# Half of a first weight group moved from ScalarE's DMA queue to the head of GpSimd's

## The chip, the cores and the metric

The kernel runs on one core of a Trainium2 chip. A core has five engines that run side by side: TensorE (matrix products), VectorE, ScalarE, GpSimd and SyncE (SP), and 16 DMA engines that move data between the device memory (HBM) and the on-chip memory (SBUF). Transfers are issued by SP, ScalarE (ACT) and GpSimd (POOL), each through a queue of its own. The metric is the device time of one execution in microseconds; before the change it is 84.93 us, the median of 7 runs (84.66 to 85.0).

## The reference

```python
batch, dim_i, dim_j, dim_k = 32, 256, 256, 128     # all float32
np.einsum('bi,bj,kij->bk', x, y, weight)
```

For every batch row b and every k the result is the bilinear form x[b] · weight[k] · y[b]. The weight is 128 x 256 x 256 float32, 33.6 MB, and is used once; x, y and the output are small.

## The kernel before

The weight is cut into G = 32 groups g. A group holds the four k with k = kk * 32 + g, kk = 0 to 3, laid out over the 128 partitions so that a partition holds eight (IC = 8) neighbouring rows i of one k, each of 256 elements j. In float32 that is 8 KB per partition and 1 MB per group. TensorE forms, for each group, the sum over i of x[b,i] * weight[k,i,j]: eight matmul steps, one per row ic, with a block matrix `xblk[:, ic]` (x spread so that the 32 batch rows meet the four k separately) as the stationary operand and the group's row ic, 256 columns, as the moving one. The result for a group is 128 x 256 float32 in PSUM, half a bank. VectorE multiplies it by y and sums over j, which gives one column of the output buffer `acc`.

Groups are worked in six units (`UNITS`) of 16, 8, 4, 2, 1 and 1 groups. Unit 0 takes the even groups and fills all eight PSUM banks; it runs its rows from ic = 7 down to 0, the next unit up, and so on. Unit 1 may start when VectorE has read unit 0's banks; units 2, 3 and 4 take banks that unit 1 does not use, and unit 5 (group 31) takes unit 1's first bank again.

The matmuls read bfloat16 from `w_sb`. Two ways lead there. Groups 0 and 16 (`FIRST`) come as plain float32 into `w_f`, group 0 through SP's queue and group 16 through ScalarE's (L134), and ScalarE casts each in two halves (L178). All the other groups come through GpSimd's queue with the cast done by the DMA itself (L120), in the order of `LOADS`: (8, 24), then (4, 12, 20, 28), then all of 2, 6, 10, ..., then unit 1's eight groups, unit 2's four, unit 3's two, group 15, and group 31 in four pieces of 4, 2, 1 and 1 rows. One transfer, y, is put between the second and third (`sw.insert(2, ...)`, L127). x goes through ScalarE's queue ahead of group 16 (L130). Every transfer has a semaphore of its own (`s_w`, `s_f`, `s_x`, `s_y`); a matmul waits for the semaphore of the load that holds its row (`sem_of`), the first time it is needed.

The order is written out by hand: the issues of all these transfers are moved to the very beginning of the program, ahead of the barrier that starts the engines (SP's and ScalarE's before anything else, GpSimd's after its start-up constants). After that GpSimd makes an identity matrix (L168, L169); VectorE repeats and transposes x (L192, L198), makes a mask from the identity (L205) and from both the block matrix (L210), then repeats and transposes y into `y4` (L219 to L227). TensorE waits for all four casts and the block matrix before its first matmul, then follows the units. At the end SP writes `acc` out, and GpSimd and SP clear the semaphores.

Of the kernel before, what the change touches and what calls it, by code (L numbers as in the profile page):

```python
# [15 lines left out]
)  # L16

LOADS = (
    ((8, 24), 0, 8),
    ((4, 12, 20, 28), 0, 8),  # L20
    (tuple(range(2, 32, 4)), 0, 8),
# [8 lines left out]
)  # L30

FIRST = (0, 16)
BANKS = 8


@with_exitstack
def kernel(
# [7 lines left out]
    nc = tc.nc  # L45
# [8 lines left out]
    _, J = y.shape  # L54
# [3 lines left out]
    IC = I // IP  # L58
# [7 lines left out]
    def sbuf(name, shape, dtype):  # L66
        return nc.alloc_sbuf_tensor(name, shape, dtype).ap()

    def rows_of(groups):


        step = G // len(groups)
        assert all(g == groups[0] + n * step for n, g in enumerate(groups))
        v = weight.rearrange("(u s) (ip ic) j -> s ip u (ic j)", s=step, ic=IC)
        return v[groups[0]]

    def w_of(groups):
        at = [place_of[g] for g in groups]
        step = at[1] - at[0] if len(at) > 1 else 1
        assert all(a == at[0] + n * step for n, a in enumerate(at))  # L80
        return w_sb[:, at[0]:at[-1] + 1:step, :]

    w_sb = sbuf("w_sb", [P, G, IC * J], bf16)
    w_f = sbuf("w_f", [P, len(FIRST), IC * J], f32)
    x_sb = sbuf("x_sb", [B, I], f32)
    y_sb = sbuf("y_sb", [B, J], f32)
# [9 lines left out]
    acc = sbuf("acc", [P, G], f32)  # L96
    ps = nc.alloc_psum_tensor("ps", [P, BANKS, 2, J], f32).ap()


    s_w = [nc.alloc_semaphore(f"w{n}") for n in range(len(LOADS))]  # L100
    sem_of = {
        (g, ic): s
        for s, (groups, lo, hi) in zip(s_w, LOADS) for g in groups for ic in range(lo, hi)
    }
    s_f = [nc.alloc_semaphore(f"f{g}") for g in FIRST]
    s_x = nc.alloc_semaphore("x")
    s_y = nc.alloc_semaphore("y")
# [11 lines left out]
    sw = [  # L119
        nc.gpsimd.dma_start(  # L120
            out=w_of(groups)[:, :, lo * J:hi * J],
            in_=rows_of(groups)[:, :, lo * J:hi * J],
        ).then_inc(s, 16).ins
        for (groups, lo, hi), s in zip(LOADS, s_w)
    ]

    sw.insert(2, nc.gpsimd.dma_start(out=y_sb, in_=y).then_inc(s_y, 16).ins)  # L127

    hw = [
        nc.scalar.dma_start(out=x_sb, in_=x).then_inc(s_x, 16).ins,  # L130
    ]
    for n, (g, queue) in enumerate(zip(FIRST, (nc.sync, nc.scalar))):
        hw.append(
            queue.dma_start(  # L134
                out=w_f[:, n:n + 1, :], in_=rows_of((g,)),
            ).then_inc(s_f[n], 16).ins
        )
    for ins in [*hw, *sw]:
# [10 lines left out]
    for blk in blocks:  # L149
# [20 lines left out]
        out=ident, in_=ident, compare_op=mybir.AluOpType.not_equal, fill=1.0,  # L170
# [3 lines left out]

    for n, g in enumerate(FIRST):
        for h in range(2):
            lo, hi = h * IC * J // 2, (h + 1) * IC * J // 2
            c = act.copy(out=w_sb[:, place_of[g], lo:hi], in_=w_f[:, n, lo:hi])  # L178
            if h == 0:
                c._wait_ge(s_f[n], 16)  # L180
            c.then_inc(s_act, 1)
# [4 lines left out]
    def done(ins):  # L186
# [6 lines left out]
        out=x_rep,  # L193
        in_=x_sb.rearrange("b (ip ic) -> b ic ip", ic=IC).unsqueeze(3)
        .to_broadcast([B, IC, IP, KK]),
    )._wait_ge(s_x, 16))
    for q in range(Q):
        c = v.transpose(  # L198
            out=xt[q * 32:(q + 1) * 32, :, :],
            in_=x_rep[:, :, q * IP // Q:(q + 1) * IP // Q, :],  # L200
# [5 lines left out]
        out=mask, in_=ident.rearrange("p (ip kk) -> p kk ip", kk=KK), axis=AX, op=add,  # L206
    )._wait_ge(s_pool, 2))

    for kk in range(KK):
        c = v.tensor_scalar(  # L210
            out=xblk[:, :, :, kk], in0=xt, scalar1=mask[:, kk:kk + 1],
# [8 lines left out]
        out=yt, in_=y_sb.rearrange("b (jb j) -> b jb j", j=32),  # L220
    )._wait_ge(s_y, 16))
    t = done(v.tensor_copy(  # L222
        out=y_rep, in_=yt.unsqueeze(3).to_broadcast([B, J // 32, B, KK]),
    )._wait_ge(s_dve, t))
    BQ = B // Q
    for q in range(Q):
        c = v.transpose(  # L227
            out=y4[q * 32:(q + 1) * 32, :].rearrange("p (jb j) -> p jb j", j=32),
            in_=y_rep[:, :, q * BQ:(q + 1) * BQ, :],
# [13 lines left out]

    pe.wait_ge(s_act, 2 * len(FIRST))
    pe.wait_ge(s_dve, t_x)
    at_dve = t_x
    n_pe = 0
    freed = [0] * BANKS
    landed = set()
    p0 = bank = 0  # L250
    held = None
    for u, unit in enumerate(UNITS):

        n_g = len(unit)
        n_b = (n_g + 1) // 2
        if bank + n_b > BANKS:
            bank = 0
# [8 lines left out]
        for n_step, (ic, h) in enumerate(steps):  # L266
            n = n_g // n_b
# [25 lines left out]
        if n_g > 1:  # L293
            t = done(v.tensor_tensor(  # L294
                out=prod, in0=sums, in1=y4.unsqueeze(1).to_broadcast([P, n_g, J]), op=mult,
# [3 lines left out]
                out=acc[:, unit[0]:unit[-1] + 1:unit[1] - unit[0]], in_=prod, axis=AX, op=add,  # L299
            )._wait_ge(s_dve, t))  # L300
        else:
            done(v.tensor_tensor_reduce(  # L302
                out=prod[:, 0, :], in0=sums[:, 0, :], in1=y4, scale=1.0, scalar=0.0,
# [44 lines left out]
```

## Time and profile before

| | |
|---|---|
| median of 7 runs | 84.93 us (84.66 to 85.0) |
| the profiled execution, and its span | 84.57 us, 83.3 us |
| TensorE busy / VectorE / ScalarE / GpSimd | 32.0 / 25.1 / 5.2 / 8.8 us |
| GpSimd's DMA queue (q0) | 4432 packets, 15.76 MB written |
| ScalarE's queue and SP's (q10, q1) | 192 and 288 packets, 1.08 and 1.07 MB written |
| read from HBM | 33.62 MB |
| issue to landing: group 0 by SP / group 16 by ScalarE / y by GpSimd | 4.8 / 8.1 / 19.6 us |
| GpSimd's issues of weight transfers | 11, at 1.06 to 9.15 us, 702 ns each in the mean |
| ScalarE's casts | 4, 1040 ns each, 7.34 to 11.22 us |
| first matmul | 41.77 us |

Times are counted from the first instruction of the span. Busy time of the engines is their compute instructions; on GpSimd the page counts the issuing of its DMAs too. GB/s and MB of a queue are bytes written, so for a casting transfer they are half of what is read. PE stands for TensorE, DVE for VectorE, ACT for ScalarE, POOL for GpSimd. L numbers are lines of the kernel before.

### The profile page before, as it was taken

Reading aid. Unit: us, or ns where it says so; the run is one execution under the profiler, and the core shown is the slowest. Engines: PE = TensorE matmul, PEld = TensorE weight load, DVE = VectorE, ACT = ScalarE, POOL = GpSimd, SP = SyncE. Lnnn points to the kernel's source line nnn. Section 1 sums busy time; section 2 is a strip of 40 time slices with the busy share of each in tenths; the row PEclk is TensorE's granted clock in tenths of the full one; section 3 lists DMA queues with packets and bytes.
Section 4 is the critical chain, followed back from the end, with each engine's and each line's share of the span. In section 5 each row is a group of like instructions: output and inputs, shape, how many; then the busy total and the mean of one; then the engine's idle time right before and its main releaser. Section 6 shows DMA issues by size and latency. Waiting matters only on the chain.

```text
span 83.3 us, 257 instructions
## 1 busy us (share of the span) xinstructions
PE 32.0 (38%) x136; PEld 4.2 (5%) x43; DVE 25.1 (30%) x28; ACT 5.2 (6%) x5; POOL 8.8 (11%) x18
## 2 busy tenths in 40 slices
PE   0000000000000000000099999994039997884780
PEld 0000000000000000000000000000000100112330
DVE  0009450000291000000000000005999602999732
ACT  0009930000000000000000000000000000000000
POOL 5999600000000000000000000000000000000000
PEclk9999999999999999999999999999975999999999
DMA  3999999999999999999999999999999999999980
GB/s 122 417 362 285 214 211 220 216 213 209 228 214 214 209 216 216 220 214 213 211 213 220 218 211 213 216 213 220 216 213 209 216 216 218 214 211 213 201 118 8
DMA packets 4912, 17.91 MB, mean 215 GB/s; under 512 B 384, under 2 KB 800, under 8 KB 4656
## 3 DMA queue, kind: packets, MB, share of 16 engines
q0 software_dynamic: 4432, 15.76, 94.5%
q10 hardware_dynamic: 192, 1.08, 3.4%
q1 hardware_dynamic: 288, 1.07, 3.3%
HBM read 33.62 MB, written 0.02 MB: 404 GB/s over the span
## 4 chain that ended last, share of the span: by engine, by line
DMA 46%; PE 39%; DVE 6%; another core or an unknown queue 3%; POOL 3%; issue 2%; POOLq 0%
DMA w_sb<-in_weight_dram 46%; PE ps L237 39%; DVE tmp L294 5%; POOL w_sb L120 2%; POOL y_sb L127 1%; DVE tmp L302 1%; POOL const-float32-0.0 L332 0%; POOLq L332 0%; POOL const-uint8-127 L332 0%; POOL const-float32-1.0 L332 0%; DVE acc L302 0%
## 5 line engine op out<-in xcount | busy, mean ns | idle before, releaser
L237 PE MATMUL ps<-w_sb,xblk 128*128 128x512 bf16 (+1 forms) x136 | 32.0, 392 | 49.2 <-DMA w_sb<-in_weight_dram 44.6
L294 DVE TENSOR_TENSOR tmp<-ps,y 128x4096 f32<-128x4096 f32 (+3 forms) x4 | 8.6, 2155 | 36.7 <-PE ps L237 36.7
L298 DVE TENSOR_REDUCE acc<-tmp 128x16 f32<-128x4096 f32 (+3 forms) x4 | 8.6, 2154 | 0.1
L237 PEld LDWEIGHTS ps<-w_sb,xblk 128*128 128x128 bf16 x43 | 4.2, 100 | 76.9 <-DMA w_sb<-in_weight_dram 42.6
L120 POOL DMA_DIRECT2D w_sb<-in_weight_dram x11 | 7.6, 702 | 0.6 <-issue 0.6
L178 ACT CAST w_sb<-w_f 128x1024 bf16<-128x1024 f32 x4 | 3.9, 1040 | 0.0
L219 DVE STREAM_TRANSPOSE yt<-y_sb 32x256 f32<-32x256 f32 x1 | 0.4, 432 | 10.8 <-DMA y_sb<-in_y_dram 10.8
L192 DVE COPY x_rep<-x_sb 32x1024 f32<-32x1024 f32 x1 | 0.8, 790 | 6.1 <-PEq L332 6.1
L198 DVE STREAM_TRANSPOSE xt<-x_rep 32x256 f32<-32x256 f32 x4 | 1.7, 435 | 0.1
L227 DVE STREAM_TRANSPOSE y<-y_rep 32x256 f32<-32x256 f32 x4 | 1.7, 435 | 0.1
L178 ACT ACT_TABLE_LOAD x1 | 1.3, 1283 | 6.0 <-PEq L332 6.0
L210 DVE TENSOR_SCALAR xblk<-xt,mask 128x256 bf16<-128x256 f32 x4 | 1.4, 502 | 0.0
L302 DVE CUSTOM_DVE_ANT_0 tmp<-ps,y 128x256 f32<-128x256 f32 x2 | 0.9, 426 | 1.6 <-PE ps L237 1.6
L222 DVE COPY y_rep<-yt 32x1024 f32<-32x1024 f32 x1 | 0.7, 680 | 0.0
L205 DVE TENSOR_REDUCE mask<-ident 128x4 f32<-128x128 f32 x1 | 0.4, 379 | 1.0 <-POOL ident L169 1.0
L127 POOL DMA_DIRECT2D y_sb<-in_y_dram x1 | 0.5, 537 | 0.0
L169 POOL TENSOR_SCALAR_AFFINE_SELECT ident<-ident 128x128 f32<-128x128 f32 x1 | 0.3, 287 | 0.1
L168 POOL MEMSET ident<- 128x128 f32 x1 | 0.3, 289 | 0.0
L302 DVE DVE_READ_ACCUMULATOR2_ANT acc<- 128x1 f32 x2 | 0.2, 84 | 0.0
L332 POOL MEMSET const-float32-0.0<- 128x1 f32 x1 | 0.1, 98 | 0.2 <-issue 0.2
L332 POOL MEMSET const-bfloat16-1.0<- 128x1 bf16 x1 | 0.1, 101 | 0.0
L332 POOL MEMSET const-uint8-127<- 128x1 uint8 x1 | 0.1, 101 | 0.0
(1 smaller groups left out, 0.1 us busy)
## 6 DMA issues: line engine op xcount, KB each, us to landing
w_sb<-in_weight_dram POOLq DMA_DIRECT2D x2, 4096.0 KB, 47.8
w_sb<-in_weight_dram POOLq DMA_DIRECT2D x2, 2048.0 KB, 43.1
w_sb<-in_weight_dram POOLq DMA_DIRECT2D x2, 1024.0 KB, 40.8
w_f<-in_weight_dram SPq DMA_DIRECT2D x1, 1024.0 KB, 4.8
w_f<-in_weight_dram ACTq DMA_DIRECT2D x1, 1024.0 KB, 8.1
w_sb<-in_weight_dram POOLq DMA_DIRECT2D x1, 512.0 KB, 72.0
w_sb<-in_weight_dram POOLq DMA_DIRECT2D x1, 256.0 KB, 72.6
w_sb<-in_weight_dram POOLq DMA_DIRECT2D x1, 128.0 KB, 72.8
```

What stands on the lines that cost most here:

```text
L120: nc.gpsimd.dma_start(out=w_of(groups)[:, :, lo * J:hi * J], in_=rows_of(groups)[:, :, lo * J:hi * J],).then_inc(s, 16).ins
L127: sw.insert(2, nc.gpsimd.dma_start(out=y_sb, in_=y).then_inc(s_y, 16).ins)
L178: c = act.copy(out=w_sb[:, place_of[g], lo:hi], in_=w_f[:, n, lo:hi])
L192: t = done(v.tensor_copy(out=x_rep, in_=x_sb.rearrange("b (ip ic) -> b ic ip", ic=IC).unsqueeze(3) .to_broadcast([B, IC, IP, KK]),)._wait_ ...
L198: c = v.transpose(out=xt[q * 32:(q + 1) * 32, :, :], in_=x_rep[:, :, q * IP // Q:(q + 1) * IP // Q, :],)
L210: c = v.tensor_scalar(out=xblk[:, :, :, kk], in0=xt, scalar1=mask[:, kk:kk + 1], scalar2=None, op0=mult,)
L222: t = done(v.tensor_copy(out=y_rep, in_=yt.unsqueeze(3).to_broadcast([B, J // 32, B, KK]),)._wait_ge(s_dve, t))
L227: c = v.transpose(out=y4[q * 32:(q + 1) * 32, :].rearrange("p (jb j) -> p jb j", j=32), in_=y_rep[:, :, q * BQ:(q + 1) * BQ, :],)
L237: return pe.add_instruction(mybir.InstMatmult(name=nc.get_next_instruction_name(), engine=mybir.EngineType.PE, ins=[pe.lower_ap(rhs), pe.l ...
L294: t = done(v.tensor_tensor(out=prod, in0=sums, in1=y4.unsqueeze(1).to_broadcast([P, n_g, J]), op=mult,)._wait_ge(s_pe, n_pe))
L298: done(v.tensor_reduce(out=acc[:, unit[0]:unit[-1] + 1:unit[1] - unit[0]], in_=prod, axis=AX, op=add,)._wait_ge(s_dve, t))
L302: done(v.tensor_tensor_reduce(out=prod[:, 0, :], in0=sums[:, 0, :], in1=y4, scale=1.0, scalar=0.0, op0=mult, op1=add, accum_out=acc[:, uni ...
```

## The change

Group 16's eight rows per partition are divided. Rows 0 to 3 still come as float32 through ScalarE's queue and are cast by ScalarE, in two halves of 512 elements per partition instead of 1024. Rows 4 to 7 come through GpSimd's queue with the cast in the DMA, as a new first entry of `LOADS`; all other entries follow in the old order, and y is put in at place 3 instead of 2, after the same transfers as before. Group 0 is as it was. TensorE's instructions are the same, with one more wait, on the new load's semaphore.

```diff
 LOADS = (
+    ((16,), 4, 8),
     ((8, 24), 0, 8),
     ((4, 12, 20, 28), 0, 8),
...
 FIRST = (0, 16)
+FIRST_ROWS = (8, 4)
...
-    sw.insert(2, nc.gpsimd.dma_start(out=y_sb, in_=y).then_inc(s_y, 16).ins)
+    sw.insert(3, nc.gpsimd.dma_start(out=y_sb, in_=y).then_inc(s_y, 16).ins)
...
             queue.dma_start(
-                out=w_f[:, n:n + 1, :], in_=rows_of((g,)),
+                out=w_f[:, n:n + 1, :FIRST_ROWS[n] * J],
+                in_=rows_of((g,))[:, :, :FIRST_ROWS[n] * J],
             ).then_inc(s_f[n], 16).ins
...
     for n, g in enumerate(FIRST):
         for h in range(2):
-            lo, hi = h * IC * J // 2, (h + 1) * IC * J // 2
+            half = FIRST_ROWS[n] * J // 2
+            lo, hi = h * half, (h + 1) * half
             c = act.copy(out=w_sb[:, place_of[g], lo:hi], in_=w_f[:, n, lo:hi])
```

## The prediction

> **What bounds the kernel now.** I read the waits first, then the chain that ended last, then the page's slices, then stretches of the opening microseconds. The waits, longest in total first (engine, line, what it waited for: us in total, times, longest):
>
> ```profile
> PE ps L237 <- DMA w_sb<-in_weight_dram: 44.6, 5, 41.8
> DVE tmp L294 <- PE ps L237: 36.7, 3, 31.8
> ...
> DVE yt L219 <- DMA y_sb<-in_y_dram: 10.8, 1, 10.8
> ```
>
> TensorE waits for weights, once for 41.8 us and four more times. The chain in order of time (start us, us, what) says how often the transfers come back:
>
> ```profile
> 3.18 38.54 DMA w_sb<-in_weight_dram
> 41.72 0.05 issue
> 41.77 15.30 PE ps L237 x64
> ...
> 61.63 8.68 PE ps L237 x32
> 70.30 0.71 another core or an unknown queue
> 71.01 0.04 issue
> 71.05 3.61 PE ps L237 x16
> 74.67 1.28 another core or an unknown queue
> 75.94 0.04 issue
> 75.98 1.89 PE ps L237 x8
> 77.87 0.49 another core or an unknown queue
> 78.36 0.04 issue
> 78.41 1.03 PE ps L237 x8
> 79.44 0.18 another core or an unknown queue
> 79.62 0.04 issue
> 79.66 0.60 PE ps L237 x4
> ```
>
> The "unknown queue" pieces are weight loads: TensorE's list of idle times names the weight DMA before 71.05, 75.98, 78.41 and 79.66. TensorE is idle before each load of the second half, so from 70.3 us on the stream of weights alone sets the end; 2.3 us of arithmetic and output follow the last one (81.0 to 83.3). That the stream has no slack is in the slices (the last lines of the page's second part) and the queues (packets, MB written, share of 16 engines):
>
> ```profile
> DMA  3999999999999999999999999999999999999980
> GB/s 122 417 362 285 214 211 220 216 213 209 228 214 214 209 216 216 220 214 213 211 213 220 218 211 213 216 213 220 216 213 209 216 216 218 214 211 213 201 118 8
> ...
> q0 software_dynamic: 4432, 15.76, 94.5%
> HBM read 33.62 MB, written 0.02 MB: 404 GB/s over the span
> ```
>
> The DMA engines are full from about 1.2 to 80.7 us. GB/s counts bytes written. Weights through GpSimd's queue are cast, 4 bytes read for 2 written, so 215 there is 430 read; the plain float32 loads of the two first groups write what they read. The kernel reads 33.6 MB whichever queue does it. A change pays only if it alters the rate per byte, or leaves the DMA engines idle.
>
> **What the Trainium skill says.** "DMA: Bandwidth & Descriptors", section "Issuing engines are not separate DMA queues": transfers from SP, ACT and GpSimd share the same 16 DMA engines and interleave. The trace agrees: a share of 1.01 to 1.06 with one queue or three. The same page, "Queues, rings and completion order": an engine goes round-robin between its queues, packet by packet. The trace agrees only in part. Its packet records (which no view lists) have ScalarE's rows of group 16 begin at 4.09 us, when SP's rows are all but over, though ScalarE's issue ended at 1.14; GpSimd's first packet is at 5.69, and only from there do the two alternate, until 8.08. The same page, "Latency and other measured facts": about 0.6 us to the first byte by SP or ACT and about 1 us by GpSimd. Here SP's came 0.78 us after its issue ended (0.63 to 1.41), GpSimd's 3.79 us (1.90 to 5.69). The measurement decides; what the excess is made of is the open question below.
>
> **The change, part by part.** Stretches of before (the columns are start:end, length, five engines' busy time, TensorE clock, DMA share, GB/s written):
>
> ```profile
> 2.00:2.50 0.50, 0.00 (x0) 0.00 (x0) 0.00 (x0) 0.00 (x0) 0.50 (x1) 1.00 1.01 393
> 2.50:3.00 0.50, 0.00 (x0) 0.00 (x0) 0.00 (x0) 0.00 (x0) 0.50 (x2) 1.00 1.01 410
> ```
>
> 1. *ScalarE's transfer loses 0.524 MB* (128 partitions, four rows of 1 KB). Plain loads run at 393, 410, 377, 442 in the four half-microseconds from 2.0, mean 405, and at 459, 311, 475 in the next three, mean 415. So 0.524 MB is 1.26 to 1.29 us of full engines; I take −1.28.
>
> 2. *The same 0.524 MB is read by GpSimd's queue with a cast.* The trace has that very shape, one group, four rows per partition: the first half of group 31. From the start of group 15's matmuls to the start of those for that half is 79.66 − 78.41 = 1.25 us. A whole group is 78.41 − 75.98 = 2.43, half of it 1.215. So +1.25, and the 4 KB rows cost 0.035 more than 8 KB ones.
>
> 3. *ScalarE's remaining half also has 4 KB rows.* No plain load of that shape is in the trace. The nearest price is the 0.035 of step 2; below, 0 (or a little under it, if short rows let the other queues in sooner, which frees nothing while the engines are full); above, twice that, 0.07. I take +0.04.
>
> 4. *One more issue on GpSimd*, ahead of everything in its queue. Issues of one group took 0.54 to 0.61 us, so y's and all eleven weight transfers are issued some 0.6 us later. Their data stand in line: the last issue ended at 9.15 and its data moved near 80.6. Cover 71 us, price 0; without it 0.6. The bytes ahead of each later transfer are the same in sum: 0.524 MB more in its own queue, 0.524 less in ScalarE's. So y lands near 22.1 as before (y4 is ready at 25.4, first needed at 57.1), and unit 0's last load near 41.7.
>
> 5. *Behind GpSimd's issue:* the identity (9.07 to 9.72), then mask and the block matrix on VectorE, ready at 11.5; later by 0.6, against a TensorE that starts at 41.77. The start barrier, which GpSimd leaves at 5.85 with its queue of issues, moves ScalarE's table load and casts from 6.04 to about 6.6. Group 16's two casts shrink from 1.04 us each to about half, so the last ends near 10.8 instead of 11.22. All of this has 30 us of cover: price 0, and 0.6 without it.
>
> 6. *TensorE's wait for the new load* stands on the fifth matmul of unit 0, behind a wait for a load issued three later in the same queue. It is long satisfied: 0. If unit 0 did start late, 0.71 us before unit 2 absorb it, and 1.28 more before unit 3; all later matmuls are queued behind it.
>
> 7. *One more semaphore to clear at the end*: the 24 cleared now take 0.03 us together: 0.
>
> Sum: −1.28 + 1.25 + 0.04 = +0.01 us, with ends −1.29 + 1.22 + 0 = −0.07 and −1.26 + 1.25 + 0.07 = +0.06. On the profiled execution, 84.57 us (83.3 of span and 1.3 around it), that is 84.58; the median of the runs, 84.93, lies 0.36 above it, so 84.94. A measurement of this kernel tells about 0.2%, 0.17 us, from no change.
>
> **The rivals.** All turn on the start, where step 1 takes work from ahead of GpSimd's first packet. Until 5.69 the engines live on SP's and ScalarE's packets. After the change these run out: ScalarE's rows begin at 4.09 and have eight 4 KB packets on each engine, at half of 0.309 to 0.326 us (the records' 8 KB packets) plus step 3's: 1.28 to 1.34 us, so they end near 5.4 on the first engines and 5.7 on the last, about 5.5 in the mean.
>
> *A, no gap (0.58):* what holds GpSimd's first packet back is the packets already queued ahead of it, as ScalarE's rows too waited out SP's (2.95 us after their issue ended, where SP's own took 0.78). Then it comes earlier when those are shorter: five of ScalarE's eight packets per engine stood before it (4.09 to 5.69 at 0.32), now at half the length, so about 4.9 us, with ScalarE packets left to alternate with. For it: SP and ACT not interleaving, and the fair alternation once GpSimd is in. Time 84.94, own range 84.80 to 85.10.
>
> *B, a gap at the start (0.27), the other side:* the 3.79 us are GpSimd's own latency, and its first packet stays at 5.69 (5.69 to 6.08 over the 16 engines, each of these behind a packet in progress, so ready near 5.7). The engines then idle from about 5.5 for 0.15 to 0.45 us, I take 0.25, and every later load, the last one too, is late by that: 85.19. It decides from the point where the first GpSimd packet comes later than about 5.65 us (0.17 past 5.5). For it: no engine's work stands in the way at 1.9 us but SP's, and nothing shows how long GpSimd's path takes when empty. Against it: ScalarE's equal delay.
>
> *C, a real gain (0.09):* GpSimd's stream reads 430 GB/s, plain loads 405. With neither short-row cost that is 0.07 us, 0.1%; beyond 0.17 only if the alternation of plain and cast packets from 5.7 to 8.1, now shorter, itself costs something. From 6 to 8 us the share is 1.05, as in the pure stretches, which speaks against it. Time 84.7.
>
> *D, dearer short rows (0.06):* 4 KB rows of plain and cast data taking turns run below the price of step 2. The stretch from 79 to 80 us, with rows of 1 and 2 KB only, wrote 194 GB/s against 215; that 10% over the 2.5 us of both halves would be +0.25, 85.18. Against it: rows of 4 KB alone lost 3%.
>
> **How the numbers follow.** A gives faster 0.03, same 0.51, slower 0.04; B same 0.04, slower 0.23; C faster 0.07, same 0.02; D slower 0.06. Together faster 0.10, same 0.57, slower 0.33. Range: from C's near edge, 84.75, to B's far one, 85.35.
>
> **What would show it.** In stretches of half a microsecond: the fall of GB/s below the plain rate beginning before 5.5 us (A) or a DMA share well under 0.8 between 5 and 6 (B). TensorE's first matmul at 41.7 to 41.9 (steps 1 to 4 in sum); under B at 42.0. Then 71.05, 75.98, 78.41 and 79.66 each moved by the same amount, no more. The last cast before 11.3, the block matrix near 12.1. I am wrong if the starts move by unlike amounts, or if the rate after 10 us is no longer 215.

## The result: 0.95% slower

The changed kernel takes 85.63 us in the median of 12 runs (85.5 to 86.11), against 84.93 us in 31 runs of the kernel before: a ratio of 1.0095, 95% interval 1.0082 to 1.0108. By that ratio it is slower by 0.8 us (the medians lie 0.7 apart), where no change was forecast and 85.35 us was the upper end of the range.

The profiled execution took 85.50 us, with a span of 84.2 us, 0.9 us longer than before; both profiled executions are at the fast end of their kernel's runs. The chain that ended last, in order of time (start us, us, what), shows where that comes in:

```profile
3.71 38.88 DMA w_sb<-in_weight_dram
42.60 0.05 issue
42.64 15.79 PE ps L241 x64
...
71.98 3.61 PE ps L241 x16
75.60 1.19 another core or an unknown queue
76.78 0.04 issue
76.83 1.89 PE ps L241 x8
78.71 0.53 another core or an unknown queue
79.24 0.04 issue
79.29 1.03 PE ps L241 x8
80.32 0.18 another core or an unknown queue
80.50 0.04 issue
80.54 0.60 PE ps L241 x4
```

Every start that waits for weights is late by nearly the same amount: 42.64 against 41.77 (0.87), 71.98 against 71.05 (0.93), 76.83 against 75.98 (0.85), 79.29 against 78.41 and 80.54 against 79.66 (0.88 each). So the loss was made before 42 us and then only carried along. The slices of the page put it in the first tenth of the span (a slice is 2.1 us):

```profile
DMA  4999999999999999999999999999999999999970
GB/s 136 391 230 218 212 212 218 210 218 218 218 210 218 216 212 218 218 212 216 214 212 212 218 216 212 218 218 210 218 214 212 212 218 210 218 218 210 200 114 8
...
q10 hardware_dynamic: 192, 0.56, 2.8%
```

From the fifth slice on the rate is 210 to 218 GB/s, as before. The second to fourth differ: 391, 230 and 218 where they were 417, 362 and 285. Part of that is only the way of counting, since the half of group 16 that GpSimd now casts counts half in bytes written. But ScalarE's queue (q10) moved half of its old bytes, 0.56 MB instead of 1.08, in 2.8% of the engines' time where it took 3.4%: a byte of it costs 1.6 times as much. The next lines show stretches of half a microsecond (start:end, length, busy time of five engines, TensorE clock, DMA share, GB/s written), first of the changed kernel, then of the kernel before. From here on a "row" of a transfer is what it carries for one partition, 8 KB for a whole group and 4 KB for half of one (the kernel's own rows of 256 elements are 1 KB); in the packet records, the trace's list of single DMA packets, each such row is one packet.

```profile
4.50:5.00 0.50, 0.00 (x0) 0.00 (x0) 0.00 (x0) 0.00 (x0) 0.50 (x2) 1.00 1.22 303
5.00:5.50 0.50, 0.00 (x0) 0.00 (x0) 0.00 (x0) 0.00 (x0) 0.50 (x2) 1.00 0.89 180
5.50:6.00 0.50, 0.00 (x0) 0.00 (x0) 0.00 (x0) 0.00 (x0) 0.50 (x2) 1.00 1.00 205
6.00:6.50 0.50, 0.00 (x0) 0.00 (x0) 0.00 (x0) 0.03 (x1) 0.50 (x2) 1.00 0.95 201
```

```profile
4.50:5.00 0.50, 0.00 (x0) 0.00 (x0) 0.00 (x0) 0.00 (x0) 0.50 (x2) 1.00 0.81 311
5.00:5.50 0.50, 0.00 (x0) 0.00 (x0) 0.00 (x0) 0.00 (x0) 0.50 (x1) 1.00 1.18 475
5.50:6.00 0.50, 0.00 (x0) 0.00 (x0) 0.00 (x0) 0.00 (x0) 0.50 (x2) 1.00 0.87 254
6.00:6.50 0.50, 0.00 (x0) 0.00 (x0) 0.42 (x1) 0.46 (x1) 0.50 (x2) 1.00 1.16 352
```

From 5.0 us until GpSimd's first packet at 6.07 ScalarE's 4 KB rows are alone and move at 180 to 205 GB/s, half of what its 8 KB rows moved at, with a DMA share of 0.9 to 1.0. The share counts an engine as busy while a packet is open on it, whether bytes move or not: here a full share stands beside half the bytes. In the packet records the first seven of ScalarE's 4 KB packets, which begin while SP's last are still under way, take 159 ns each; most of those from 4.9 to 6.2 us take 270 to 390 ns. Summed over all queues, the records have 0.36 to 0.39 MB less read between 4.0 and 6.5 us than before (spread over the time a packet is open, or counted at its start); at the stream's 430 GB/s that is 0.83 to 0.90 us, the whole loss.

### The profile page after: what moved, and what is told of

Read it like the earlier page. It is cut to its first block, busy times and chain, and to the rows that moved or that the text cites. A ratio compares the mean times of both kernels' runs of the same rounds, so it can differ in the third digit from the quotient of the medians.

```text
span 84.2 us, 258 instructions
## 1 busy us (share of the span) xinstructions
PE 32.5 (39%) x136; PEld 4.3 (5%) x43; DVE 25.2 (30%) x28; ACT 4.3 (5%) x5; POOL 9.4 (11%) x19
## 4 chain that ended last, share of the span: by engine, by line
DMA 46%; PE 39%; DVE 6%; POOL 3%; another core or an unknown queue 3%; issue 2%; POOLq 0%
DMA w_sb<-in_weight_dram 46%; PE ps L241 39%; DVE tmp L298 5%; POOL w_sb L122 3%; POOL y_sb L129 1%; DVE tmp L306 1%; POOL const-float32-0.0 L336 0%; POOLq L336 0%; POOL const-uint8-127 L336 0%; POOL const-float32-1.0 L336 0%; DVE acc L306 0%
## 5 line engine op out<-in xcount | busy, mean ns | idle before, releaser
L241 PE MATMUL ps<-w_sb,xblk 128*128 128x512 bf16 (+1 forms) x136 | 32.5, 397 | 49.6 <-DMA w_sb<-in_weight_dram 44.9
L122 POOL DMA_DIRECT2D w_sb<-in_weight_dram x12 | 8.1, 690 | 0.6 <-issue 0.6
L182 ACT CAST w_sb<-w_f 128x1024 bf16<-128x1024 f32 (+1 forms) x4 | 3.0, 828 | 0.0
```

Source lines behind the costliest of these rows:

```text
L122: nc.gpsimd.dma_start(out=w_of(groups)[:, :, lo * J:hi * J], in_=rows_of(groups)[:, :, lo * J:hi * J],).then_inc(s, 16).ins
L241: return pe.add_instruction(mybir.InstMatmult(name=nc.get_next_instruction_name(), engine=mybir.EngineType.PE, ins=[pe.lower_ap(rhs), pe.l ...
```

## The experiments

In the edits below "..." stands for lines left out, and what follows a # is a note of this text.

The theory, R: a transfer from SP's or ScalarE's queue is handed to the engines row by row, at a rate that does not depend on the row's length and that 8 KB rows only just fill. With 4 KB rows half of the engines' capacity stays empty until GpSimd's data come, at about 6 us. The rivals: G, GpSimd's new first transfer slows ScalarE's packets; F, short rows move at a fixed low bandwidth; S, GpSimd's start is late by itself.

**One part alone: the row length.** The kernel before, with GpSimd's queue untouched and group 16 sent by ScalarE as two transfers of four rows.

```diff
-    for n, (g, queue) in enumerate(zip(FIRST, (nc.sync, nc.scalar))):
+    for n, (g, queue, lo, hi) in enumerate((
+        (0, nc.sync, 0, 2 * half), (16, nc.scalar, 0, half), (16, nc.scalar, half, 2 * half),
+    )):
...
```

> The kernel before, with group 16 still wholly through ScalarE's queue, but as two transfers of four rows each; GpSimd's queue is untouched. Theory R (rows of SP's and ScalarE's transfers are handed out at about 19 to 20 ns each, 305 ns per engine, whatever their length, so that 4 KB rows leave the DMA engines half used until GpSimd's data begin): ScalarE's packets take about 300 ns from 4.3 us on, the stretch from 4.5 to 5.7 runs near 200 GB/s, the first matmul comes 0.7 to 0.9 us later than before, 85.6 to 85.8 us. Rival G (the slow packets of the changed kernel come from GpSimd's new first transfer taking turns with them): 4 KB packets at about 160 ns, 84.9 to 85.0 us.

Measured: 85.83 us, ratio 1.0117 (1.0096 to 1.0137), at the upper end of what R gave. Its stretches:

```profile
4.50:5.00 0.50, 0.00 (x0) 0.00 (x0) 0.00 (x0) 0.00 (x0) 0.50 (x2) 1.00 1.13 295
5.00:5.50 0.50, 0.00 (x0) 0.00 (x0) 0.00 (x0) 0.00 (x0) 0.50 (x1) 1.00 1.00 213
5.50:6.00 0.50, 0.00 (x0) 0.00 (x0) 0.00 (x0) 0.00 (x0) 0.50 (x2) 1.00 1.00 213
```

The same picture as in the changed kernel, without any change on GpSimd. The cost is in the short rows, and G falls as its main cause.

The second of the two transfers shows the same rows again, from 6.6 us on, in turns with GpSimd's 8 KB rows. The stretch from 8 to 9 us:

```profile
8.00:9.00 1.00, 0.00 (x0) 0.00 (x0) 0.72 (x2) 1.00 (x2) 1.00 (x3) 1.00 1.06 283
```

In the records 35 packets of ScalarE's and 34 of GpSimd's start in it, so about half of the 283 GB/s is written by a cast and counts half: some 420 GB/s are read, close to the stream's 430. ScalarE's 4 KB packets take 172 ns each there. So neither the length of a row as such nor the gaps of 4 KB that half a group leaves between its rows in HBM make a packet slow; what is slow is short rows on ScalarE's queue while that queue is alone.

**The other queue.** Group 0, SP's, is halved instead of group 16.

```diff
-    ((16,), 4, 8),
+    ((0,), 4, 8),
...
-FIRST_ROWS = (8, 4)
+FIRST_ROWS = (4, 8)
```

> The changed kernel with the halves exchanged: group 0, SP's, is the one with four rows by SP and four by GpSimd first; group 16 comes whole through ScalarE. Theory R: SP's 4 KB rows are slow from the start, 1.4 to 3.9 us at about 210 GB/s, then ScalarE's 8 KB rows at about 400; some 1.0 to 1.2 us lost, 85.9 to 86.2 us. Rival G: nothing of GpSimd's is under way before 2.5 us, so SP's 4 KB rows go at about 160 ns each and are over by 2.8 us, ScalarE's by 5.4 us, then a short gap until GpSimd's first packet: 85.1 to 85.4 us.

Measured: 86.16 us, ratio 1.0159 (1.0143 to 1.0174). The stretch from 2 to 3 us, here and, in the second fence, before:

```profile
2.00:3.00 1.00, 0.00 (x0) 0.00 (x0) 0.00 (x0) 0.00 (x0) 1.00 (x2) 1.00 0.82 233
```

```profile
2.00:3.00 1.00, 0.00 (x0) 0.00 (x0) 0.00 (x0) 0.00 (x0) 1.00 (x2) 1.00 1.01 401
```

It is no matter of ScalarE's queue or of the moment: SP's 4 KB rows are nearly as slow two to three microseconds earlier, and since nothing else runs until ScalarE's rows follow, the loss is larger, as R has it. In the records 107 of them start in the 2.0 us from 1.4 us, 53 in a microsecond, and 83 of these are done in 200 ns or less: the engines stand idle between them (the share is 0.82, not 1.0). So here the rows come late to the engines; they are not slow on them.

**The place in GpSimd's queue.** The half goes second, behind groups 8 and 24.

```diff
-    ((16,), 4, 8),
     ((8, 24), 0, 8),
+    ((16,), 4, 8),
```

> The changed kernel with GpSimd's half of group 16 as its second transfer, behind groups 8 and 24. Theory R: ScalarE's 4 KB rows are as slow as in the changed kernel until GpSimd's first packet: 85.5 to 85.8 us. Rival G: GpSimd's first transfer is that of before, so the cost of the new first transfer is gone: 84.9 to 85.1 us. The place itself is worth nothing by either.

Measured: 85.50 us, ratio 1.0086 (1.0069 to 1.0103), not to be told from the change's 1.0095. That the half is GpSimd's first transfer plays no part that shows.

**The dose.** Two rows and six rows by ScalarE, the rest of group 16 by GpSimd first.

```diff
-    ((16,), 4, 8),
+    ((16,), 2, 8),          # and ((16,), 6, 8)
...
-FIRST_ROWS = (8, 4)
+FIRST_ROWS = (8, 2)         # and (8, 6)
```

> The changed kernel with two of group 16's rows by ScalarE (2 KB per partition) and six by GpSimd first. Theory R, a row of ScalarE's transfer every 19.4 ns whatever its length: the engines carry 2 KB per 19.4 ns, about 105 GB/s, from 4.4 us until GpSimd's data begin at 5.9 to 6.1; three quarters of 1.7 us are lost, 1.2 to 1.4 us, 86.0 to 86.3 us. Rival F, 4 KB and shorter rows move at a fixed 205 GB/s: 0.26 MB is over by 5.6 us, some 0.6 us lost in it and up to 0.5 us of gap after it.

> The changed kernel with six rows by ScalarE (6 KB per partition) and two by GpSimd first. Theory R: 6 KB per 19.4 ns, about 315 GB/s, from 4.4 us until 5.8 to 6.0; a quarter of 1.5 us lost, 0.35 to 0.45 us, 85.2 to 85.4 us. Rival F: rows above 4 KB move at the full 400 GB/s, 84.8 to 85.0 us.

Measured: 86.07 us (1.0158, 1.0143 to 1.0173) and 85.28 us (1.0067, 1.0052 to 1.0082). One stretch of each, with ScalarE's rows nearly alone; in this order two rows, four (the change), six, and eight (before, half a microsecond earlier, as GpSimd's data come sooner there):

```profile
5.00:6.00 1.00, 0.00 (x0) 0.00 (x0) 0.00 (x0) 0.00 (x0) 1.00 (x2) 1.00 0.91 94
```

```profile
5.00:6.00 1.00, 0.00 (x0) 0.00 (x0) 0.00 (x0) 0.00 (x0) 1.00 (x2) 1.00 0.95 193
```

```profile
5.00:6.00 1.00, 0.00 (x0) 0.00 (x0) 0.00 (x0) 0.00 (x0) 1.00 (x2) 1.00 0.97 300
```

```profile
4.50:5.50 1.00, 0.00 (x0) 0.00 (x0) 0.00 (x0) 0.00 (x0) 1.00 (x2) 1.00 0.99 393
```

94, 193, 300 and 393 GB/s (17 of the 300 are GpSimd's, whose data begin at 5.49 us there): the bytes follow the row's length, while the DMA share stays at 0.9 to 1.0. Counted in the packet records, ScalarE's rows that start in these stretches are 46, 47, 46 and 48 in a microsecond, about 21 ns a row, at 2, 4, 6 and 8 KB. That is R's central claim, and it leaves no room for F. At 8 KB the count can't be told from the limit of the engines themselves, whose packets of that length take 322 ns. For six rows the time lost (0.55 us) is somewhat above what R gave.

**The same short rows at another time.** Groups 0 and 16 stay whole; group 24 is halved, its four rows by ScalarE coming behind group 16, when GpSimd's data are under way.

```diff
-    ((16,), 4, 8),
-    ((8, 24), 0, 8),
+    ((8,), 0, 8),
+    ((24,), 4, 8),
...
-FIRST = (0, 16)
-FIRST_ROWS = (8, 4)
+FIRST = (0, 16, 24)
+FIRST_ROWS = (8, 8, 4)
...
-    for n, (g, queue) in enumerate(zip(FIRST, (nc.sync, nc.scalar))):
+    for n, (g, queue) in enumerate(zip(FIRST, (nc.sync, nc.scalar, nc.scalar))):
```

> Groups 0 and 16 whole by SP and ScalarE as in the kernel before; it is group 24 that is halved, four rows by ScalarE behind group 16 (and cast by ScalarE), four by GpSimd behind group 8. The same 128 rows of 4 KB, but at a time when GpSimd's data are under way. Theory R, short rows cost only where nothing else fills the engines: the packets alternate with GpSimd's and the rate stays near 430 GB/s read, 84.7 to 85.0 us. Rival F, 4 KB rows of ScalarE's queue are dear wherever they stand: 85.4 to 85.7 us.

Measured: 85.05 us, ratio 1.0029 (1.0015 to 1.0043). F's 85.4 to 85.7 is out; R's 84.7 to 85.0 is just missed. Most of the cost is gone when another queue fills the engines, but 0.25 us stay. In the records the 4 KB rows take 185 ns each in the mean, from 8.4 to 11.9 us. The stretch from 9 to 10 us:

```profile
9.00:10.00 1.00, 0.00 (x0) 0.00 (x0) 0.07 (x1) 1.00 (x2) 0.93 (x3) 1.00 1.02 233
```

By the same count as above (29 packets of ScalarE's, 28 of GpSimd's) that is about 350 GB/s read, where the first experiment had 420 with the same mixture. The short rows are not what is slower: they take 172 ns here too, but GpSimd's 8 KB rows take 406 instead of 322. Only from 10 to 11.5 us, where GpSimd's rows are short as well, do ScalarE's take longer, 193 ns. What slows GpSimd's packets was not found, so it isn't shown that the 0.25 us are the price of short rows.

**What GpSimd's first packet waits for.** Group 16 wholly by GpSimd; then groups 0 and 16 both, with no weights on SP's or ScalarE's queue at all.

```diff
-    ((16,), 4, 8),
+    ((16,), 0, 8),          # the second kernel: ((0, 16), 0, 8)
...
-FIRST = (0, 16)
-FIRST_ROWS = (8, 4)
+FIRST = (0,)                # the second kernel: ()
+FIRST_ROWS = (8,)           # the second kernel: ()
...
```

> Group 16 comes whole through GpSimd, as its first transfer and with the cast there; ScalarE's queue carries x alone and ScalarE casts group 0 only. This asks what GpSimd's first packet waits for. If it is its own path (S), it comes at 5.7 to 6.1 us again, the DMA engines idle from about 4.4 us until then, and the kernel takes 86.2 to 86.6 us. If it waits for ScalarE's and SP's rows to be handed out (R with a shared hand-out), it comes at about 4 to 4.5 us, and the kernel takes 84.8 to 85.1 us.

> No weights through SP's or ScalarE's queue: groups 0 and 16 both come through GpSimd as its first transfer, ScalarE casts nothing, and only x goes by ScalarE's queue. This shows when GpSimd's first packet comes with nothing in its way. Theory S, its own path takes 4.6 to 5 us from the issue at 1.06: at 5.7 to 6 us, 89 us in all (4.5 us of empty engines less the 0.3 us that the cast stream saves over 2 MB). If what it waits for is rows of SP and ScalarE ahead of it: at 2.5 to 3.5 us, 85.7 to 86.8 us.

Measured: 86.31 us (1.0155, 1.0106 to 1.0205; its runs were 86.35, 85.43, 86.37 and 86.26) and 85.93 us (1.0129, 1.0105 to 1.0153). The stretches of the second:

```profile
1.50:2.50 1.00, 0.00 (x0) 0.00 (x0) 0.00 (x0) 1.00 (x2) 1.00 0.00 0
2.50:3.50 1.00, 0.00 (x0) 0.00 (x0) 0.00 (x0) 1.00 (x3) 1.00 0.94 115
3.50:4.50 1.00, 0.00 (x0) 0.00 (x0) 0.00 (x0) 1.00 (x2) 1.00 1.07 209
```

With nothing in its way GpSimd's first packet is at 2.61 us and the stream is at its rate from about 3.4. So S is out: from the end of its first issue (1.91) the path takes 0.7 us, near the 1 us that the Trainium skill gives ("DMA: Bandwidth & Descriptors", "Latency and other measured facts"), and the 5.69 of before was a wait on the other queues' rows. With SP's 128 rows alone ahead of it (the first of the two kernels) the first packet is at 4.23, as SP's rows end; but the time came out on S's side, because the first packets are slow:

```profile
4.00:5.00 1.00, 0.00 (x0) 0.00 (x0) 0.00 (x0) 0.00 (x0) 1.00 (x2) 1.00 1.38 180
5.00:6.00 1.00, 0.00 (x0) 0.00 (x0) 0.00 (x0) 0.00 (x0) 1.00 (x2) 1.00 0.61 119
6.00:7.00 1.00, 0.00 (x0) 0.00 (x0) 0.49 (x1) 0.53 (x1) 1.00 (x3) 1.00 0.98 172
```

From 5 to 6 us GpSimd's queue, alone now, writes 119 GB/s, not 215. In the records seven of its first two dozen packets stay open for 1.5 to 1.8 us, the others for 0.3 to 0.7. So the question had a third answer, which neither expectation held: an early first packet and a slow start behind it. One of this kernel's four runs was 0.9 us faster than the rest; no profile shows that one, and what holds these packets was not found.

**A gain that R seemed to offer.** If x's 32 rows of 1 KB took their turn in one hand-out ahead of SP's, moving them would free 0.6 us. The kernel before, with x behind group 16 in ScalarE's queue, and with x by GpSimd ahead of y:

```diff
-        nc.scalar.dma_start(out=x_sb, in_=x).then_inc(s_x, 16).ins,
...
+    hw.append(nc.scalar.dma_start(out=x_sb, in_=x).then_inc(s_x, 16).ins)                # x last
+    sw.insert(2, nc.gpsimd.dma_start(out=x_sb, in_=x).then_inc(s_x, 16).ins)             # or by GpSimd
```

> The kernel before with x's transfer behind group 16's in ScalarE's queue instead of ahead of it. Theory R: x's 32 rows of 1 KB take 32 x 19.4 ns = 0.6 us of the hand-out while the DMA engines have little else, from 1.2 to 1.8 us; behind group 16 they fall into a time when GpSimd's data fill the engines. Gain 0.2 to 0.5 us, 84.4 to 84.7 us. Without a shared hand-out of rows, x is 32 KB, 0.08 us of the engines: no difference that can be measured, 84.8 to 84.95 us. VectorE gets x some 7 us later, under the same 30 us of cover as before.

> The kernel before with x taken from ScalarE's queue and issued by GpSimd just ahead of y. x and with it the block matrix come at about 22 to 28 us, still before TensorE's first matmul at 41.8. Theory R: the same gain as with x last in ScalarE's queue, 0.2 to 0.5 us, 84.4 to 84.7 us; without a shared hand-out no difference.

Measured: 84.98 us (1.0026, 1.0015 to 1.0036) and 84.96 us (1.0026, 1.0016 to 1.0036): both a little slower, which neither side of the expectation had. The start of the kernel with x last:

```profile
1.00:1.50 0.50, 0.00 (x0) 0.00 (x0) 0.00 (x0) 0.00 (x0) 0.45 (x1) 1.00 0.76 164
1.50:2.00 0.50, 0.00 (x0) 0.00 (x0) 0.00 (x0) 0.00 (x0) 0.50 (x2) 1.00 0.41 98
```

SP's first weight packet is at 1.41 us with x ahead, behind or elsewhere, so x's rows held nothing up; they went out in the time before SP's arrived. The version of R with one hand-out for both queues is not supported by this at the start. What remains of R is the rate per row, and that only for loads of 128 rows of 2 to 8 KB, as the dose had them. At 21 ns a row x's 32 rows of 1 KB would start over 0.67 us; they start within 0.25 to 0.36 us in eight of the ten kernels that send x ahead through ScalarE's queue (0.73 to 0.75 in the other two). The output's 128 rows of 128 bytes, written to HBM through SP's queue at the end, would need 2.7 us; they start within 0.22 us in every kernel. So R is no rate of rows in general. Why both kernels are 0.25% slower was not settled: the stretch from 1.5 to 2.0 us is emptier here (98 GB/s; 303 before), but it is nearly as empty (115 to 164) in several of the kernels above that have x ahead. No version beat the kernel before.

## Why the prediction was wrong

*The failed step is the third: "ScalarE's remaining half also has 4 KB rows", priced at +0.04 us with 0.07 as the upper bound.* Measured: 128 packets at 275 ns in the mean, 2.20 us on each of the 16 engines, where step 3 had 1.28 to 1.34. That is +0.9 us and the whole difference. The price was taken from the first half of group 31, which has rows of the same length but comes by GpSimd's queue, and GpSimd's rows of that shape took 172 ns each in the changed kernel too. What limits these rows of SP's and ScalarE's, a count per microsecond, could not show in the kernel before: there all their weight rows were 8 KB, and 48 of those in a microsecond are 393 GB/s, which looks like an engine at its limit. The bound of twice the neighbour's price took a different queue's price for the same unknown.

*Steps 1 and 2 were sound in bytes but not in time.* GpSimd's half took about what was said: its 128 packets at 172 ns are 1.38 us on each engine, or some 1.30 at the stream's share of 1.06 (an estimate; said 1.25). But of the 1.28 us that step 1 takes off ScalarE's queue only 0.4 came back: its packets took 2.20 us on each engine, where before they took 2.61. It had 128 rows before and after.

*Steps 4 to 7 held.* The last issue on GpSimd ended 0.55 us later (9.70), the block matrix was ready at 12.1 (said 12.1), the last cast at 10.79 (said 10.8), and none of that was on the path.

*Rival A, the forecast, was half right about GpSimd's start.* What holds its first packet is rows queued ahead, as the kernel without them shows (2.61 us). But A let it come at 4.9 because these rows had become shorter, and it came at 6.07. Shorter rows did not bring it sooner: it came at 6.05 behind 2 KB rows, 5.49 behind 6 KB, 5.69 behind 8 KB. The number of rows alone does not set it either, since with 384 rows on the two queues it came at 5.58 (the first experiment) and 5.48 (group 24 halved). What sets the moment stays open.

*Rival B did not occur.* There is no gap: ScalarE's packets last until 6.9 and overlap GpSimd's; and the 3.79 us of before were not GpSimd's own. *C, a gain, did not occur either. D named dearer short rows,* but with a tenth of slowdown while both queues take turns. The cost was made while ScalarE's short rows ran alone; the 0.25 us of the kernel with group 24 halved are of D's size, but not shown to be its cause.

*The test I had set was too coarse.* I would have told a gap by a DMA share under 0.8; the share was 0.89 to 1.0 while half of the bytes were missing. GB/s showed it. My other sign, a GB/s below the plain rate before 5.5 us, did appear, and would have been read for A. What I had named as signs of being wrong did not come: the starts moved by like amounts (0.85 to 0.93 us), and the rate after 10 us is 215 still.

## What to carry to other kernels

A load through SP's or ScalarE's queue that has to fill the DMA engines by itself should keep the bytes per partition row long; here 8 KB rows were just enough, and halving the rows took only 0.4 of 2.6 us off the time of their packets. Take a price only from a row of the same queue as well as the same shape, and read the DMA share together with the bytes. The same short rows went at full speed (172 ns) where they took turns with another queue's data, and the kernel that placed them there lost 0.25 us instead of 0.8 to 1.3. All this was seen in the first microseconds of the program, with one or two transfers on a queue; a longer stream of short rows through SP's or ScalarE's queue alone was not run.

## What the runs showed of the hardware that was not expected

- ScalarE's rows, alone, started at 46 to 48 in a microsecond at 2, 4, 6 and 8 KB (94, 193, 283 and 393 GB/s); SP's 4 KB rows at 53. That these rows are handed out one by one is an explanation that fits: with SP's the engines stood idle between packets of mostly under 200 ns, and ScalarE's 4 KB packets took 159 ns behind SP's and 172 in turns with GpSimd's, against 270 to 390 alone. It does not hold for all rows, since x's and the output's started faster. The Trainium skill ("Perfetto Trace Analysis", "DMA Instruction — HWDGE (DVE, Sync)") speaks of one block that makes the descriptors for both issuing sequencers (DVE and Sync in its title; a note there names SP and ScalarE). ScalarE's rows starting only as SP's end (4.09 us in the kernel before) agrees; x's rows, which held nothing up, do not show it. No run here shows the source of the rate directly.
- GpSimd's queue does not show this: its 4 KB rows took 172 ns in the changed kernel, and 8 KB rows 324.
- GpSimd's first packet comes 0.7 us after the end of its first issue when the other queues carry no weights, 2.5 us behind 128 rows of SP's, and 3.8 (before) and 4.3 (changed) with 256 rows on both. Over all kernels with 256 or more it is 3.4 to 4.3.
